# A second k-group by seven products in the second feed-forward, its last weight sum added by a DMA

## The chip, the cores and the metric

The kernel runs on one core of one Trainium2 chip. The metric is the device time of one execution in microseconds, the median over several runs; before the change it is 2688.29 us (three runs, 2687.02 to 2688.56). Engine names are those of the profile: PE is TensorE, DVE is VectorE, ACT is ScalarE, POOL is GpSimd, and SP is the engine whose queue issues the weight loads.

## The reference, cut to what matters

The program is two transformer-like blocks on one sequence of 256 tokens with width 2048, all in float32: sliding-window attention and a SwiGLU feed-forward; then a gated hybrid mixer, a cross attention and a second feed-forward, and a last norm. The change touches the up side of both feed-forwards. In the first:

```
silu(h @ w_gate) * (h @ w_up)        # then @ w_down
```

In the second, `w_up` holds both halves (2 x 5632 columns), a causal three-tap convolution over the tokens comes between, and the halves are then gated:

```
u = h @ w_up
u = causal_conv(u, conv_w) + conv_b
gate, val = u[..., :D_FF_2], u[..., D_FF_2:]
(silu(gate) * val) @ w_down
```

So each feed-forward needs, for one block of 512 columns, two products with the same activations: a left one (gate) and a right one (up, or val), each for two halves of 128 tokens. That is a 2 x 2 arrangement of outputs, and if the sum over the 2048 inputs is cut in two as well, a 2 x 2 by 2 x 2 matrix product.

## The kernel before, in words

**Tiles.** The weights stand in HBM as units of 1 MB: 512 inputs (four k-tiles of 128 rows) by 512 columns. The 2048 inputs are four k-groups of 512, numbered 0 to 3; a unit is one k-group of one column block. SP loads units in a fixed order (`plan`) into four buffers (`RAW = 4`), each loaded again once its last reader is done. A float32 product is made of three passes of a narrower type, so each weight is split first: half a unit (128 x 1024 elements) goes through ACT (`wh`, line 235, a cast) and then DVE (`wl`, line 236, the remainder). Such a split half is a task. Tasks are written three ahead of PE (`AHEAD = 3`), and there are five buffers each for `wh` and `wl` (`WBUF = 5`), so the cast of a task waits until PE is done with the task five before it. `mm` (lines 276 to 282) issues three matmuls with a moving size of 512 columns for each product of one k-tile.

**Seven products.** `pair` computes the left and the right column block together. A normal k-group there takes two units, four tasks and 48 matmuls. For the k-groups listed in `SEVEN1` (first feed-forward) and `SEVEN2` (second) the four half units b11, b21 (left) and b12, b22 (right) and sums of them make seven tasks of two k-tiles and 42 matmuls, as in Strassen's scheme with few additions. The sums of weights are made in place by `form` on DVE, the sums of activations once by `differences`, and the sums of results by the `add` calls in `pair` after the last such group (index 3). The seven products are numbered 0 to 6 here, as `form`'s index `i`. Product 6 uses b21 after its sum, product 2 uses b21 as loaded.

**Order.** Each feed-forward has eleven column blocks; the first goes through `gemm`, the other ten through `pair`. Between two calls of `pair` stand four units of the down projection (`ffn_steps`, `PARTS`). Side work (the convolution, transposes, the split of the hidden block) is written as generators that are stepped once per k-tile or product (`tick`). The order on PE is the written one. On ACT, DVE, POOL and SP the compiler's scheduler orders instructions by when it expects them to be ready, so their order in the profile is not always that of the source; once placed, each engine works its queue in order. PSUM has four banks for `acc` (the four outputs p2 to p5 of a pair, or two outputs of a `gemm`), three for `aux` (o1 and o6 of a pair, transposes) and one for `po` (o7). A `gemm` after a pair takes `acc` banks as they come free.

POOL computes only `power` (line 445) before the change and issues no DMA.

Of the kernel before, what the change touches and what calls it, by code (L numbers as in the profile page):

```python
# [14 lines left out]
ALU = mybir.AluOpType  # L15
# [19 lines left out]
WBUF = 5  # L35
AHEAD = 3
PARTS = ((0,), (1, 2), (3, 4), (5, 6), (7, 8), (9, 10))
SEVEN1, SEVEN2 = (1, 3), (3,)
BRANCH = ((0,), (1,), (2, 3))
LEVELS = (64, 32, 16, 8, 4, 2, 1)  # L40

# [42 lines left out]
class _Net:  # L84
# [87 lines left out]
    def plan(self):  # L172
# [13 lines left out]
        def ffn(gate, up, off, down, seven):  # L186
            for c, n, ks in self.ffn_steps():
                if n is not None:
                    add([U(down, n, ks)])
                elif c:  # L190
                    pair(U(gate, c), U(up, c + off), seven)
                else:
                    add([U(gate, c), U(up, c + off)], True)
            add([U(down, n, PARTS[-1]) for n in range(4)])
# [51 lines left out]
    def form(self, u, i):  # L246

        nc = self.nc
        self.load_ahead(u + 2)
        b12, b22, b11, b21 = (self.raws[u + j][:, 2 * i:2 * i + 2] for j in range(2) for i in range(2))  # L250
        if i == 2:
            nc.vector.tensor_sub(b22, b22, b12)
            nc.vector.tensor_sub(b12, b12, b11)
            nc.vector.tensor_add(b11, b11, b22)
        if i == 5:
            nc.vector.tensor_sub(b21, b21, b11)
        return (b22, b11, b21, b11, b12, b22, b21)[i]

    def task(self):

# [40 lines left out]
    def differences(self, acts, seven):  # L301


        nc = self.nc
        out = []
        for g, z in enumerate(acts):
            h, l = z = self.need(z)
            f = self.s4([128, 4, 256])
            nc.vector.tensor_add(f, h.bitcast(F32), l.bitcast(F32))
            p, q = f[:, :, 0:128], f[:, :, 128:256]  # L310
            yield 2
            if g not in seven:
                h, l = (self.s2([128, 4, 128], F32R) for _ in range(2))
                nc.vector.tensor_sub(p, p, q)
                nc.scalar.copy(h, p)
                nc.vector.tensor_sub(l, p, h.bitcast(F32))
            else:
                s = self.s4([128, 8, 128])
                nc.vector.tensor_add(s[:, 0:2], q[:, 0:2], q[:, 2:4])
                nc.vector.tensor_sub(s[:, 2:4], s[:, 0:2], p[:, 0:2])  # L320
                nc.vector.tensor_sub(s[:, 4:6], p[:, 0:2], q[:, 0:2])
                nc.vector.tensor_sub(s[:, 6:8], p[:, 2:4], s[:, 2:4])
                yield 1
                h, l = (self.s4([128, 8, 128], F32R) for _ in range(2))
                nc.scalar.copy(h, s)
                nc.vector.tensor_sub(l, s, h.bitcast(F32))
            out.append((h, l))
            yield 2
        return out

    def pair(self, left, right, acts, diffs, seven):

        nc = self.nc
        add = nc.vector.tensor_add
        acts = [self.need(z) for z in acts]
        p2, p4, p5, p3 = (self.bank(tag="acc") for _ in range(4))  # L340
        used = set()

        def product(o, z, k, t, stop):
            h, l = self.task()
            for i in range(2):
                self.mm(o, z, k + i, t, (h[:, i], l[:, i]), id(o) not in used, stop and i == 1)
                used.add(id(o))
            self.tick()

        o1 = None  # L350
        for g in range(len(acts)):
            A, S = acts[g], diffs[g]
            if g not in seven:
                for units in (right, left):
                    outs = ((p2, A, 0), (p4, A, 1)) if units is left else ((p5, A, 1), (p3, S, 0))
                    for k, w in enumerate(self.weights(units[g])):
                        for o, z, t in outs:
                            self.mm(o, z, k, t, w, id(o) not in used, False)
                            used.add(id(o))
                        self.tick()  # L360
                continue
            assert self.stream[self.used:self.used + 2] == [right[g], left[g]]
            self.used += 2
            if o1 is None:
                o1, o6, o7 = self.bank(), self.bank(), self.bank(tag="po")
            end = g == seven[-1]
            product(p3, S, 6, 0, end)
            product(o1, A, 0, 0, end)
            if end:
                u, a, b, c = (self.s2([128, 512]) for _ in range(4))  # L370
                nc.scalar.copy(u, o1)
            product(p2, A, 2, 0, end)
            if end:
                add(a, p2, u)
                yield a
            product(o6, S, 2, 0, end)
            if end:
                add(u, o6, u)
            product(p5, S, 0, 0, end)
            if end:  # L380
                add(b, p5, u)
                add(b, p3, b)  # L382
                yield b
            product(o7, S, 4, 0, end)
            if end:
                add(u, o7, u)
            product(p4, A, 2, 1, end)
        add(c, p4, u)
        add(u, p5, u)
        yield c  # L390
        yield u


    def group(self):
# [937 lines left out]
```

## Time and profile before

| | |
|---|---|
| median of three runs | 2688.29 us |
| the profiled execution's own time | 2686.66 us |
| its span, first to last instruction | 2684.5 us |
| TensorE clock granted, mean | 0.999 |
| PE busy | 2657.9 us (99%) |
| DVE busy | 1890.7 us (70%) |
| ACT busy | 1424.2 us (53%) |
| POOL busy | 27.1 us (1%) |
| DMA, mean | 186 GB/s |

The profiled execution is one run; its span is 2.2 us shorter than its time. A busy PE in this profile is not PE at its peak, since matmul records overlap: a 512-column matmul is shown with 390 ns, and the step from one start to the next is what counts. Idle time of an engine that is not the bottleneck costs nothing.

### The profile page before, as it was taken

What the parts mean: (1) busy time and instruction counts of PE and PEld (TensorE: products, weight loads), DVE (VectorE), ACT (ScalarE), POOL (GpSimd) and SP (SyncE); (2) the same over time, 40 slices, a digit from 0 to 9 for tenths busy, and PEclk for the clock granted to TensorE, in tenths of its full rate; (3) what the DMA queues carried; (4) which work ended last, traced back from release to release, by engine and by line L of the source; (5) the groups of instructions that cost most, each with busy time, mean ns of one, the idle gap of its engine ahead of it and who ended that gap; (6) DMA issues with size and microseconds to landing.
All of it is one profiled execution on the core that took longest, in us unless ns stands there. A gap on an engine that the chain in (4) does not pass through costs nothing.

```text
span 2684.5 us, 31592 instructions
## 1 busy us (share of the span) xinstructions
PE 2657.9 (99%) x12352; PEld 2195.2 (82%) x12352; DVE 1890.7 (70%) x2225; ACT 1424.2 (53%) x1849; POOL 27.1 (1%) x27
## 2 busy tenths in 40 slices
PE   8999999999999999999999999999999999999998
PEld 7778888888888888888888888888878888888887
DVE  7775799888888864655545555454578877777776
ACT  6555555555555555454444555444555655555554
POOL 0100000000000000000000000000000000000000
PEclk9999999999999999999999999999999999999999
DMA  7334455555555554445555566444554555555553
GB/s 304 113 126 145 169 218 187 205 192 206 209 195 200 194 187 178 151 172 188 188 190 193 183 225 212 172 157 168 183 180 175 190 193 194 192 190 195 194 193 138
DMA packets 74086, 499.61 MB, mean 186 GB/s; under 512 B 8496, under 2 KB 9392, under 8 KB 14928
## 3 DMA queue, kind: packets, MB, share of 16 engines
q1 hardware_dynamic: 73936, 497.59, 51.4%
q8 instruction: 97, 1.59, 0.2%
q14 instruction: 53, 0.43, 0.0%
HBM read 495.46 MB, written 2.10 MB: 185 GB/s over the span
## 4 chain that ended last, share of the span: by engine, by line
PE 97%; DVE 2%; ACT 1%; POOL 0%; DMA 0%; issue 0%; SPq 0%; POOLq 0%; DVEq 0%; ACTq 0%
PE acc L280 29%; PE acc L282 29%; PE acc L281 29%; PE aux L421 2%; PE aux L282 1%; PE aux L281 1%; PE aux L280 1%; PE po L734 1%; PE po L282 1%; PE po L281 1%; PE po L280 1%; PE aux L969 0%; POOL sm L445 0%; DVE wl L236 0%; DMA raw<-in_w_qkv 0%; PE aux L695 0%
## 5 line engine op out<-in xcount | busy, mean ns | idle before, releaser
L236 DVE TENSOR_TENSOR wl<-raw,wh 128x1024 fp32r<-128x1024 f32 (+1 forms) x1012 | 1230.7, 1220 | 689.0 <-ACT wh L235 677.1
L235 ACT CAST wh<-raw 128x1024 fp32r<-128x1024 f32 (+1 forms) x1012 | 1060.2, 1051 | 1084.0 <-PE acc L282 1020.6
L280 PE MATMUL acc<-wh,s 128*128 128x512 f32 x3440 | 1364.1, 397 | 7.4 <-ACT wh L235 5.5
L282 PE MATMUL acc<-wh,s 128*128 128x512 f32 x3440 | 1342.6, 390 | 0.6 <-DVE s L404 0.6
L281 PE MATMUL acc<-wl,s 128*128 128x512 f32 x3440 | 1341.0, 390 | 0.4 <-DVE wl L236 0.4
L280 PEld LDWEIGHTS acc<-wh,s 128*128 128x128 f32 x3440 | 646.9, 188 | 145.5 <-DVE s L382 7.1
L282 PEld LDWEIGHTS acc<-wh,s 128*128 128x128 f32 x3440 | 646.2, 188 | 138.1 <-DVE s L404 1.1
L281 PEld LDWEIGHTS acc<-wl,s 128*128 128x128 f32 x3440 | 647.3, 188 | 128.2 <-DVE wl L236 1.7
L467 DVE TENSOR_TENSOR x<-acc,x 128x512 f32<-128x512 f32 x112 | 72.8, 682 | 0.0
L421 PEld LDWEIGHTS aux<-con,s 128*128 128x128 f32 x408 | 50.2, 140 | 15.7 <-issue 4.0
L421 PE MATMUL aux<-con,s 128*128 128x128 f32 x408 | 60.9, 272 | 1.8 <-DVE s L1162 1.8
L1159 ACT ACTIVATE s<-aux,vec 128x256 f32<-128x256 f32 x88 | 47.9, 560 | 12.5 <-PE aux L421 7.8
L403 ACT CAST s<-aux 128x512 fp32r<-128x512 f32 x66 | 38.4, 584 | 28.9 <-PE aux L421 18.6
L445 POOL TENSOR_TENSOR sm<-sm,mhalf 128x2 f32<-128x2 f32 (+3 forms) x22 | 26.0, 1182 | 2651.0 <-DVE sm L453 2314.1
L404 DVE TENSOR_TENSOR s<-aux,s 128x512 fp32r<-128x512 f32 x66 | 44.6, 687 | 11.5 <-ACT s L403 10.3
L408 ACT ACTIVATE s<-aux,vec 128x256 fp32r<-128x256 f32 x80 | 37.7, 473 | 22.3 <-PE aux L421 14.2
L280 PE MATMUL aux<-wh,s 128*128 128x512 f32 x120 | 46.7, 389 | 0.0
L281 PE MATMUL aux<-wl,s 128*128 128x512 f32 x120 | 46.7, 389 | 0.0
L282 PE MATMUL aux<-wh,s 128*128 128x512 f32 x120 | 46.7, 389 | 0.0
L409 DVE SCALAR_TENSOR_TENSOR s<-aux,vec,s 128x256 fp32r<-128x256 f32 x80 | 38.3, 482 | 6.5 <-ACT s L408 5.3
L1160 DVE SCALAR_TENSOR_TENSOR s<-aux,vec,s 128x255 f32<-128x255 f32 x88 | 41.0, 478 | 2.4 <-ACT s L1159 0.2
L1162 DVE SCALAR_TENSOR_TENSOR s<-aux,vec,s 128x254 f32<-128x254 f32 x88 | 40.0, 477 | 1.1
(195 smaller groups left out, 1309.1 us busy)
## 6 DMA issues: line engine op xcount, KB each, us to landing
raw<-in_w_up SPq DMA_DIRECT2D x132, 1024.0 KB, 4.8
raw<-in_w_dn SPq DMA_DIRECT2D x88, 1024.0 KB, 4.8
raw<-in_w_in SPq DMA_DIRECT2D x64, 1024.0 KB, 4.8
raw<-in_w_gate SPq DMA_DIRECT2D x44, 1024.0 KB, 4.8
raw<-in_w_ckv SPq DMA_DIRECT2D x32, 1024.0 KB, 4.7
raw<-in_w_qkv SPq DMA_DIRECT2D x19, 1024.0 KB, 5.4
raw<-in_w_o SPq DMA_DIRECT2D x16, 1024.0 KB, 4.7
raw<-in_w_br SPq DMA_DIRECT2D x16, 1024.0 KB, 4.7
```

The source lines that it names most:

```text
L235: nc.scalar.copy(h[:, m], raw[:, m])
L236: nc.vector.tensor_sub(l[:, m], raw[:, m], h[:, m].bitcast(F32))
L280: nc.tensor.matmul(o, ah[:, k, s], h, start=first, stop=False)
L281: nc.tensor.matmul(o, ah[:, k, s], l, start=False, stop=False)
L282: nc.tensor.matmul(o, al[:, k, s], h, start=False, stop=last)
L403: nc.scalar.copy(h[:, k0:k0 + n], src)
L404: nc.vector.tensor_sub(l[:, k0:k0 + n], src, h[:, k0:k0 + n].bitcast(F32))
L421: self.nc.tensor.transpose(b[:, j, t * 128:t * 128 + 128], srcs[t][:, (k + j) * 128:(k + j) * 128 + 128], self.ident)
L467: nc.vector.tensor_add(xs[t], pss[t], xs[t])
L1159: nc.scalar.activation(y[:, j], b[:, j], AF.Identity, bias=bb, scale=w2)
L1160: nc.vector.scalar_tensor_tensor(y[:, j, 1:256], b[:, j, 0:255], w1, y[:, j, 1:256], op0=ALU.mult, op1=ALU.add)
L1162: nc.vector.scalar_tensor_tensor(y[:, j, 2:256], b[:, j, 0:254], w0, y[:, j, 2:256], op0=ALU.mult, op1=ALU.add)
```

## The change

- `SEVEN2` becomes `(1, 3)`: in the second feed-forward k-group 1 goes by seven products too, as it did in the first.
- `form` makes its sums with plus signs: b22 gets b12 added, b12 gets b11 added (index 2), then b11 gets the new b22 added (now at index 3). The last sum, b21 plus the new b11, is no DVE instruction any more but a DMA issued by POOL that adds b11 into b21, both in SBUF (128 x 1024 float32, 512 KB). This holds for both feed-forwards.
- The order of the products 4 and 5 changes: now o7 (with b22) is product 4 and p5 (with b12) is product 5; p5 was product 4 before.
- `differences` has other signs. The sums of results have other signs, and the last of them are ordered anew: after p5 come b, b with p3, u with o7, d; after p4 one sum remains where there were two.

```diff
-SEVEN1, SEVEN2 = (1, 3), (3,)
+SEVEN1, SEVEN2 = (1, 3), (1, 3)
...
         if i == 2:
-            nc.vector.tensor_sub(b22, b22, b12)
-            nc.vector.tensor_sub(b12, b12, b11)
+            nc.vector.tensor_add(b22, b22, b12)
+            nc.vector.tensor_add(b12, b12, b11)
+        if i == 3:
             nc.vector.tensor_add(b11, b11, b22)
-        if i == 5:
-            nc.vector.tensor_sub(b21, b21, b11)
-        return (b22, b11, b21, b11, b12, b22, b21)[i]
+            nc.gpsimd.dma_start(b21, b11, accum_op=ALU.add)
+        return (b22, b11, b21, b11, b22, b12, b21)[i]
...
                 s = self.s4([128, 8, 128])
-                nc.vector.tensor_add(s[:, 0:2], q[:, 0:2], q[:, 2:4])
+                nc.vector.tensor_sub(s[:, 0:2], q[:, 0:2], q[:, 2:4])
                 nc.vector.tensor_sub(s[:, 2:4], s[:, 0:2], p[:, 0:2])
                 nc.vector.tensor_sub(s[:, 4:6], p[:, 0:2], q[:, 0:2])
-                nc.vector.tensor_sub(s[:, 6:8], p[:, 2:4], s[:, 2:4])
+                nc.vector.tensor_add(s[:, 6:8], p[:, 2:4], s[:, 2:4])
...
-                u, a, b, c = (self.s2([128, 512]) for _ in range(4))
+                u, a, b, d = (self.s2([128, 512]) for _ in range(4))
...
+            product(o7, S, 4, 0, end)
             product(p5, S, 0, 0, end)
             if end:
-                add(b, p5, u)
+                nc.vector.tensor_sub(b, p5, u)
                 add(b, p3, b)
                 yield b
-            product(o7, S, 4, 0, end)
-            if end:
                 add(u, o7, u)
+                nc.vector.tensor_sub(d, p5, u)
             product(p4, A, 2, 1, end)
-        add(c, p4, u)
-        add(u, p5, u)
-        yield c
+        add(u, p4, u)
         yield u
+        yield d
```

## Rows read from the trace of the kernel before

**Rows 1.** The page's first part: busy time, share, instructions of each engine.
```profile
PE 2657.9 (99%) x12352; PEld 2195.2 (82%) x12352; DVE 1890.7 (70%) x2225; ACT 1424.2 (53%) x1849; POOL 27.1 (1%) x27
```

**Rows 2.** Waits, whole execution: who <- for whom, us in total, times, longest.
```profile
PEld acc L280 <- DVE s L382: 7.1, 20, 0.4
```

**Rows 3.** Busy us (instructions) PE, PEld, DVE, ACT, POOL, clock, DMA: one period each.
```profile
747.20:810.90 63.70, 63.70 (x286) 52.50 (x285) 54.55 (x54) 34.20 (x35) 0.00 (x0) 1.00 0.53 198
2235.90:2301.90 66.00, 66.00 (x299) 54.38 (x298) 52.42 (x64) 37.03 (x44) 0.00 (x0) 1.00 0.53 192
```

**Rows 4.** Timeline of PE (start us, us): product 1, then the down projection.
```profile
2203.85 0.39 PE L280 MATMUL aux<-wh,s 128*128 128x512 f32 x1
...
2212.01 0.39 PE L280 MATMUL acc<-wh,s 128*128 128x512 f32 x1
```

**Rows 5.** DVE groups in one period of the second feed-forward: busy, mean ns.
```profile
L236 DVE TENSOR_TENSOR wl<-raw,wh 128x1024 fp32r<-128x1024 f32 x27 | 32.7, 1221 | 12.7 <-ACT wh L235 12.5
...
L256 DVE TENSOR_TENSOR raw<-raw 128x1024 f32<-128x1024 f32 x1 | 1.2, 1225 | 0.0
```

**Rows 6.** Timeline of DVE: k-group 3 of one pair, second feed-forward.
```profile
2198.96 1.22 DVE L236 TENSOR_TENSOR wl<-raw,wh 128x1024 fp32r<-128x1024 f32 x1
...
2207.45 1.22 DVE L236 TENSOR_TENSOR wl<-raw,wh 128x1024 fp32r<-128x1024 f32 x1
...
2210.32 0.69 DVE L381 TENSOR_TENSOR s<-acc,s 128x512 f32<-128x512 f32 x1
2210.91 1.22 DVE L236 TENSOR_TENSOR wl<-raw,wh 128x1024 fp32r<-128x1024 f32 x1
2212.05 0.69 DVE L382 TENSOR_TENSOR s<-acc,s 128x512 f32<-128x512 f32 x1
...
2213.25 1.22 DVE L236 TENSOR_TENSOR wl<-raw,wh 128x1024 fp32r<-128x1024 f32 x1
```

**Rows 7.** Timeline of ACT, the same group: casts of tasks 6 to 9.
```profile
2205.89 2.00 ACT L235 CAST wh<-raw 128x1024 fp32r<-128x1024 f32 x2
...
2208.41 2.18 ACT L235 CAST wh<-raw 128x1024 fp32r<-128x1024 f32 x2
```

**Rows 8.** Timeline of SP's queue, the same pair: weight loads issued.
```profile
2186.03 5.73 SPq L215 DMA_DIRECT2D raw<-in_w_dn  x2
...
2206.72 2.30 SPq L215 DMA_DIRECT2D raw<-in_w_dn  x2
```

**Rows 9.** Timeline, first feed-forward, k-group 1: split of task 2, cast and product 6.
```profile
627.03 1.22 DVE L236 TENSOR_TENSOR wl<-raw,wh 128x1024 fp32r<-128x1024 f32 x1
...
633.53 1.05 ACT L235 CAST wh<-raw 128x1024 fp32r<-128x1024 f32 x1 [0.30 <-PE aux L282]
...
638.73 0.39 PE L280 MATMUL acc<-wh,s 128*128 128x512 f32 x1
```

**Rows 10.** Timeline, second feed-forward: first tasks of k-group 1, DVE and PE.
```profile
2305.82 2.36 DVE L236 TENSOR_TENSOR wl<-raw,wh 128x1024 fp32r<-128x1024 f32 x2
...
2312.82 0.39 PE L280 MATMUL acc<-wh,s 128*128 128x512 f32 x1
```

**Rows 11.** DMA issues: count, KB each, median us from issue to landing.
```profile
raw<-in_w_up SPq DMA_DIRECT2D x132, 1024.0 KB, 4.8
...
out<-x SPq DMA_DIRECT2D x8, 256.0 KB, 2.4
...
s<-in_g_final SPq DMA_DIRECT2D x2, 512.0 KB, 6.9
```

**Rows 12.** Timeline of POOL: three of its `power` instructions.
```profile
35.95 0.70 POOL L445 TENSOR_TENSOR sm<-sm,mhalf 128x2 f32<-128x2 f32 x1 [35.51 <-DVE sm L453]
...
85.85 2.54 POOL L445 TENSOR_TENSOR sm<-sm,mhalf 128x8 f32<-128x8 f32 x1 [26.17 <-DVE sm L614]
...
97.98 1.64 POOL L445 TENSOR_TENSOR sm<-sm,mhalf 128x8 f32<-128x8 f32 x1 [9.59 <-DVE sm L614]
```

**Rows 13.** DVE groups around the second feed-forward's `differences`: busy, mean ns.
```profile
L319 DVE TENSOR_TENSOR s<-s 128x256 f32<-128x256 f32 x1 | 0.4, 419 | 0.0
```

## Prediction

> **What bounds the kernel now.** I read the page's busy shares first: PE is at 99%, DVE at 70%, ACT at 53%, POOL at 1% [rows 1]. Then the waits, to see whether anything holds PE: the wait that recurs is for the sum of line 382, twenty times, 7.1 us in all and never over 0.4 us [rows 2]. Then one period (a pair and the four units of the down projection behind it) of each feed-forward: PE is busy through all of both, 63.7 us in the first and 66.0 us in the second, at full clock, while DVE has 54.55 and 52.42 us of work in them [rows 3]. So time falls only if PE gets fewer matmuls, or DVE, ACT or the new DMA comes to hold PE up. How far that is away is read from the timelines of single groups.
>
> **What is removed on PE.** From the first matmul of product 1 to the first of the down projection there are six products of six matmuls, 36 starts in 2212.01 - 2203.85 = 8.16 us, 0.2267 us each and 1.36 us a product [rows 4]. A normal k-group in a pair takes 48 matmuls, a group by seven products 42. Ten pairs lose six each: 60 x 0.2267 = 13.6 us, all on the path.
>
> **DVE and ACT, second feed-forward.** Per pair the new group has seven tasks in place of four: three more splits of 1.22 us. Sums of weights: four on DVE before, twice three now. That is five more instructions, 5 x 1.22 = 6.1 us [rows 5], so DVE goes from 52.4 of 66.0 to 58.5 of 64.6 us, 91%; ACT gets three casts of 1.05 us. In the first feed-forward DVE loses two sums a pair, to 52.1 of 63.7. PE waits for no DVE total there, so that gains nothing; the sums of results stay seven. I cost the totals at nothing, since splits run ahead of PE by up to five tasks; what is late next is local, below.
>
> **The accumulating DMA.** POOL can issue it when task 2 is split (it reads b21) and the third sum is made; product 6's cast waits for its landing, and behind that cast stand all later casts in ACT's queue, behind task 6's split all later DVE work. What is the room?
> - Group 3, both feed-forwards, 20 groups: task 2's split ends at 2198.96 + 1.22 = 2200.2, task 6's cast starts at 2205.89 [rows 6, 7]: 5.7 us. Its split started at 2207.45, 0.5 us after that cast's end. So 6.2 us cost nothing. Beyond that the DVE chain up to line 382 slides, and PE already waits for its end [rows 2]: a late microsecond costs one.
> - Group 1, first feed-forward, 10 groups: task 2's split ends at 628.25 and its cast of task 6 starts at 633.53, 5.3 us; but PE begins product 6 only at 638.73 [rows 9], so with 2.3 us for cast and split the DMA may take 8.2 us.
> - Group 1, second feed-forward, 10 groups: here DVE still works off the convolution. It begins the group's splits at 2305.82, PE begins the group at 2312.82 [rows 10]. Six instructions must pass (three splits, three sums) at 1.18 to 1.22 us, so the DMA starts at about 2313.0; product 6 is due at 2312.82 + 6 x 1.36 = 2320.98, less 2.3: the room is 5.7 us.
>
> How long it takes, no row shows; there is no DMA from POOL and none that adds. From below: a store of 256 KB, half the bytes and no second operand, lands in 2.4 us [rows 11], so not under 3. From above: two passes of a 1 MB load, 2 x 4.8, and the longest POOL instruction shown for making the transfer, 2.5 [rows 11, 12]: 12.1 us. I take the nearest: 512 KB of source and 512 KB of destination are read, the bytes of one 1 MB load, 4.8 us, and 0.7 us on POOL as its shortest instruction [rows 11, 12]: 5.5 us. It should not meet other transfers: in group 3 the loads before it are issued by 2191.8 and land 4.8 us later, the next is issued at 2206.72 [rows 8]. Two loads of 512 KB took 6.9 us each [rows 11]. At 5.5 us the cost is nothing; at 3 too; at 12.1 it is 20 x 5.9 + 10 x 6.4 + 10 x 3.9 = 221 us. POOL's queue holds nothing else there that anyone waits for.
>
> The Trainium skill prices this too: its page "DMA: Bandwidth & Descriptors", section "Anatomy of one DMA — SWDGE (gpsimd) path", gives about 2.0 us plus the bytes over 436 GB/s. By it, an estimate, 512 KB take 3.2 us, or 4.4 with both operands counted, and the sum would stay as it is.
>
> **Sums of results.** p5 moves from product 4 to 5, 1.36 us later, and the second bank of the down projection hangs on b with p3. PE ends product 5 at about 2210.7 and wants the bank at 2212.01 + 0.68 = 2212.7; before, line 382 ended at 2212.05 + 0.69 = 2212.74. Now DVE can put task 8's split where line 381 stood, at 2210.32 (its cast is done by 2209.5), then the two sums: 2211.5 to 2212.75 [rows 6, 7]. The same wait, cost nothing; it has no slack. If the wait of rows 2 went, at most its 7.1 us would be gained.
>
> **`differences`, once.** Group 1's form makes four sums of 0.42 us and one of 1.22 where two of 0.68 were [rows 6, 13]: 1.5 us more on DVE. Between 0 and 1.5 us; I take 0.8.
>
> **Sum.** 13.6 - 0.8 = 12.8 us off the profiled execution's 2686.66 (span 2684.5 and 2.2 around it): 2673.9. The median lies 1.6 us higher: 2675.5, say 2676.
>
> **Rivals.**
> - *The sum lands late (slower).* One mechanism: task 6 waits, ACT and DVE stand behind it, and line 382's successor comes late to PE. With X us from issue to landing the loss is 20 x (X - 6.2) + 10 x (X - 5.7), and it decides from X = 6.5, where it eats the 12.8. At X = 7.3 it is 38 us: 2714. For it: two loads of 512 KB took 6.9 us [rows 11], and adding may not run at the rate of a load. Against: the DMA engines are free there.
> - *DVE holds up POOL while it makes the transfer.* The same `power` instruction of 128x8 took 1.64 us once and 2.54 another time [rows 12], so something on this core can delay POOL by 0.9 us. Then X is 6.4, the loss 20 x 0.2 + 10 x 0.7 = 11, and the time about 2687. The Trainium skill, "SBUF — State Buffer", section "Who interferes with whom", has the cause: a DVE instruction with two SBUF inputs contends with a GpSimd instruction that reads SBUF, not with one that only writes. The rows of `power`, which reads, would fit its first half; whether making descriptors counts as writing only, no row shows.
> - *A split gets between the sums.* If the scheduler puts task 9's split ahead of b with p3 (its cast is done by 2210.6 [rows 7]), the bank comes at 2213.9, 1.15 us later, in 20 pairs: 23 us, 2698.6. Against: before, both line 382 and the sum after it went ahead of that split, which came at 2213.25 [rows 6].
> - *It doesn't do what it says*: DVE at 91% falls behind in the second feed-forward wherever a wait leaves it idle, and PE stands 1 to 2 us a pair: 2686 to 2696.
>
> **How the numbers follow.** The forecast has 0.50; the late sum 0.20; POOL held up 0.15; the split between 0.10; DVE behind 0.05. A change under 0.2% (5.4 us) can't be told from none. Faster takes the forecast and a third of POOL's case, 0.55; same, half of POOL's and edges of the others, 0.14; slower the rest, 0.31. The forecast's own range is 2668 (the old wait gone) to 2681 (X at 6.0 to 6.2 in places). To hold 8 in 10 it must reach into the late sum, to X of 7.2: 2712; below 2668 no term reaches.
>
> **What would show it.** PE periods of 64.6 us in the second feed-forward and 63.7 in the first, no new wait of PE. POOL to landing under 5.7 us. In each group of seven, ACT's cast of task 6 not waiting for a DMA, or by less than 0.5 us. Line 382's successor ending within 0.1 us of PE's need. DVE at 58.5 us a period. The prediction is wrong if PE waits behind task 6, or if the landing takes over 6.5 us; and the gain itself is mis-sized if the step between matmuls is no longer 0.227 us.

## The result, and the profile after it

The changed kernel takes 2707.19 us (median of 4 runs, 2706.48 to 2709.59) against 2688.36 us for the kernel before (2687.02 to 2688.56): ratio 1.0073, interval 1.0055 to 1.009. It is slower by 18.8 us, where 12.8 us less was forecast. The profiled execution took 2706.85 us, its span is 2705.1 us and the mean granted clock 0.999, as before; the clock has a small part in it, 1.6 us in one place, told below. From line 390 or so on, line numbers are one lower than before.

The first part of the page after (it answers [rows 1]):

```profile
PE 2649.4 (98%) x12292; PEld 2184.4 (81%) x12292; DVE 1920.6 (71%) x2258; ACT 1450.5 (54%) x1879; POOL 62.0 (2%) x67
```

The 60 matmuls are gone, and with them 8.5 us of PE's busy time. The span is 20.6 us longer all the same: PE now stands more often. The waits of PE and of its weight loads, whole execution (who <- for whom, us in total, times, longest), say where; they answer [rows 2]:

```profile
PEld acc L280 <- DVE s L383: 33.1, 20, 2.2
...
PE acc L280 <- DVE s L383: 24.6, 20, 1.8
...
PE aux L420 <- DVE s L1161: 4.5, 3, 1.7
```

Line 383 is `add(b, p3, b)`, line 382 of before. The wait for it still comes 20 times, once a pair, but up to 2.2 us (1.8 by PE's own row) where it was never over 0.4. The third row has grown too, from 1.8 us in one wait before: transposes of the convolution, held by VectorE. Next the periods, which answer [rows 3] (busy us and instructions of PE, PEld, DVE, ACT, POOL, clock, DMA share, GB/s): one of the first feed-forward, one of the second, and one short one of the second, from its pair 2 to pair 3, which was not looked at before the prediction:

```profile
737.85:802.71 64.86, 63.80 (x285) 52.51 (x284) 52.24 (x52) 34.28 (x35) 1.74 (x2) 1.00 0.61 210
2257.36:2323.56 66.20, 64.76 (x294) 53.26 (x292) 57.90 (x69) 39.70 (x47) 1.72 (x2) 1.00 0.62 207
2059.71:2118.57 58.86, 54.64 (x247) 44.05 (x246) 52.46 (x65) 35.50 (x44) 1.72 (x2) 1.00 0.58 197
```

The first feed-forward, whose matmuls did not change, takes 1.16 us more a period. In the second, 64.6 us were forecast; PE has 64.76 us of busy time in a period of 66.20. The third row has the same stretch in the kernel before beside it here:

```profile
2047.16:2102.30 55.14, 55.14 (x254) 45.35 (x252) 47.62 (x59) 32.89 (x41) 0.00 (x0) 1.00 0.52 191
```

There PE had no idle time, and six matmuls less should have made it 53.8 us. It takes 58.86, with 52.46 us of work on VectorE.

What happens at a pair's end is seen in the timeline of DVE (start us, us, line, operation, times in a row), group 3 of one pair; it answers [rows 6]:

```profile
2427.31 2.35 DVE L236 TENSOR_TENSOR wl<-raw,wh 128x1024 fp32r<-128x1024 f32 x2
2429.58 0.68 DVE L382 TENSOR_TENSOR s<-acc,s 128x512 f32<-128x512 f32 x1
2430.18 1.21 DVE L236 TENSOR_TENSOR wl<-raw,wh 128x1024 fp32r<-128x1024 f32 x1
2431.32 0.68 DVE L383 TENSOR_TENSOR s<-acc,s 128x512 f32<-128x512 f32 x1
```

and in that of PE at the same place, which answers [rows 4]:

```profile
2430.37 0.39 PE L281 MATMUL acc<-wl,s 128*128 128x512 f32 x1
2430.60 0.39 PE L282 MATMUL acc<-wh,s 128*128 128x512 f32 x1
2432.05 0.50 PE L280 MATMUL acc<-wh,s 128*128 128x512 f32 x1 [1.06 <-DVE s L383]
2432.39 0.39 PE L281 MATMUL acc<-wl,s 128*128 128x512 f32 x1
```

The matmul of 2432.05 is the first into the down projection's second bank, p3's old one. By the step of 0.2267 us it was due at 2430.83; it starts 1.22 us late, when the sum of line 383 is done. Between the two sums of b stands a split (2430.18). Without it line 383 would have ended at about 2430.9.

The accumulating DMA, the page's row of its issues and two of POOL's instructions (they answer [rows 11, 12]):

```profile
raw<-raw POOLq DMA_DIRECT2D x40, 512.0 KB, 4.5
```

```profile
2400.76 0.86 POOL L256 DMA_DIRECT2D raw<-raw  x1 [45.95 <-DVE raw L255]
2419.69 0.86 POOL L256 DMA_DIRECT2D raw<-raw  x1 [18.07 <-DVE wl L236]
```

In the median it lands 4.5 us after its issue: under the 5.5 us that I took and the room of 5.7 to 8.2 that I gave it; 38 of the 40 take 4.48 to 4.81 us, the longest 6.37. In the main the forecast feared the wrong part of the change. But in five of the 20 groups 3 ScalarE's cast of task 6 waits 0.7 to 1.1 us for this landing, as in pair 1 of the second feed-forward:

```profile
2041.41 2.00 ACT L235 CAST wh<-raw 128x1024 fp32r<-128x1024 f32 x2 [1.03 <-DMA raw<-raw]
...
2048.98 0.50 PE L280 MATMUL acc<-wh,s 128*128 128x512 f32 x1 [1.74 <-DVE s L383]
```

In these five the sum of line 383 comes 0.4 to 0.7 us later still than in the pair above, 2.9 us in all (pairs 1, 2, 3 and 5 of the second feed-forward, where the DMA is issued later against PE, and pair 9 of the first, where it takes the 6.37 us).

From the starts of the first matmul of a unit the time can be laid out by stage. The start-up (first weights) differs by up to 2 us from one profiled execution to the next, in every kernel, and is left out. A pair here is the stretch from its first product to that of the next pair; pairs 1 and 2 have two units of the down projection behind them, the others four. Pair 10 has no next pair and is left out.

| us | before | changed | difference |
|---|---|---|---|
| first feed-forward and what lies ahead of it | 970.15 | 982.33 | +12.2 |
| the stages between, and the second feed-forward's first column block | 1003.79 | 1003.79 | 0 |
| second feed-forward, pair 1 | 58.72 | 59.33 | +0.6 |
| pair 2 | 55.13 | 58.86 | +3.7 |
| pair 3 | 67.55 | 72.96 | +5.4 |
| pairs 4 to 9, each | 66.04 | 65.8 (one 66.2) | -0.2 |

In pair 3 of the changed kernel the clock was lower for a short while (the same columns as in the periods above):

```profile
2168.30:2172.00 3.70, 3.70 (x11) 2.89 (x10) 3.61 (x5) 2.15 (x3) 0.00 (x0) 0.54 0.73 259
```

For most of this stretch the trace grants the lower of the clock's two levels, 1.2 GHz, and the matmuls step 0.43 us instead of 0.227: 1.6 of pair 3's 5.4 us. 1.5 us before it, PE had ended a wait of 1.78 us for line 383; in pair 2 it waited 1.70 us there and kept the clock, so what brought it down is not shown. The profile of the kernel before has no such place outside its first and last microseconds.

Two questions follow. Is it the order of the two sums (and not the DMA) that costs over 1 us a pair? And what takes the rest of the 9.7 us in the second feed-forward's first three pairs?

### The profile page after: what moved, and what is told of

It is laid out like the page before. It is cut to its first block, busy times and chain, and to the rows that moved or that the text cites. A ratio compares the mean times of both kernels' runs of the same rounds, so it can differ in the third digit from the quotient of the medians.

```text
span 2705.1 us, 31717 instructions
## 1 busy us (share of the span) xinstructions
PE 2649.4 (98%) x12292; PEld 2184.4 (81%) x12292; DVE 1920.6 (71%) x2258; ACT 1450.5 (54%) x1879; POOL 62.0 (2%) x67
## 4 chain that ended last, share of the span: by engine, by line
PE 85%; DVE 8%; issue 3%; DMA 2%; ACT 1%; POOL 0%; SPq 0%; DVEq 0%; POOLq 0%; ACTq 0%
PE acc L280 26%; PE acc L282 25%; PE acc L281 25%; DVE wl L236 4%; PE aux L420 2%; DMA raw<-raw 2%; PE aux L282 1%; PE aux L281 1%; PE aux L280 1%; ACT wh L235 1%; PE po L733 1%; DVE s L378 1%; DVE s L382 0%; DVE s L383 0%; PE aux L968 0%
## 5 line engine op out<-in xcount | busy, mean ns | idle before, releaser
L236 DVE TENSOR_TENSOR wl<-raw,wh 128x1024 fp32r<-128x1024 f32 (+1 forms) x1042 | 1259.9, 1219 | 680.9 <-ACT wh L235 669.5
L235 ACT CAST wh<-raw 128x1024 fp32r<-128x1024 f32 (+1 forms) x1042 | 1081.6, 1050 | 1058.5 <-PE acc L282 924.1
L280 PE MATMUL acc<-wh,s 128*128 128x512 f32 x3360 | 1333.7, 397 | 31.8 <-DVE s L383 24.6
L282 PE MATMUL acc<-wh,s 128*128 128x512 f32 x3360 | 1311.9, 390 | 0.6 <-DVE s L403 0.6
L281 PE MATMUL acc<-wl,s 128*128 128x512 f32 x3360 | 1311.0, 390 | 1.6 <-DVE wl L236 1.6
L280 PEld LDWEIGHTS acc<-wh,s 128*128 128x128 f32 x3360 | 632.2, 188 | 168.3 <-DVE s L383 33.1
L282 PEld LDWEIGHTS acc<-wh,s 128*128 128x128 f32 x3360 | 631.6, 188 | 135.7 <-DVE s L403 1.1
L256 POOL DMA_DIRECT2D raw<-raw x40 | 34.8, 870 | 1258.3 <-DVE wl L236 692.4
L281 PE MATMUL aux<-wl,s 128*128 128x512 f32 x160 | 62.6, 391 | 0.4 <-DVE wl L236 0.4
L282 PE MATMUL aux<-wh,s 128*128 128x512 f32 x160 | 62.3, 389 | 0.0
L280 PE MATMUL aux<-wh,s 128*128 128x512 f32 x160 | 62.3, 389 | 0.0
L1158 ACT ACTIVATE s<-aux,vec 128x256 f32<-128x256 f32 x88 | 47.7, 560 | 13.6 <-PE aux L420 7.8
L255 DVE TENSOR_TENSOR raw<-raw,raw 128x1024 f32<-128x1024 f32 x40 | 48.9, 1223 | 1.1
L252 DVE TENSOR_TENSOR raw<-raw 128x1024 f32<-128x1024 f32 x40 | 48.9, 1222 | 1.0
```

The costliest lines, as they stand in the source:

```text
L235: nc.scalar.copy(h[:, m], raw[:, m])
L236: nc.vector.tensor_sub(l[:, m], raw[:, m], h[:, m].bitcast(F32))
L252: nc.vector.tensor_add(b22, b22, b12)
L280: nc.tensor.matmul(o, ah[:, k, s], h, start=first, stop=False)
L281: nc.tensor.matmul(o, ah[:, k, s], l, start=False, stop=False)
L282: nc.tensor.matmul(o, al[:, k, s], h, start=False, stop=last)
```

## The experiments

Theory A: p3's bank is freed too late, since the sum that frees it waits for p5, which comes one product later, and a split stands in between. Theory B: the accumulating DMA. Theory C: VectorE has too much to do. All runs were timed in turn with the kernel before.

**1. p3's sum ahead of p5's**

```
             add(u, o6, u)
+            nc.vector.tensor_sub(b, p3, u)
...
-            nc.vector.tensor_sub(b, p5, u)
-            add(b, p3, b)
+            add(b, p5, b)
```

> The changed kernel (2707.2 us), with the sum that reads p3 moved ahead: b = p3 - u right behind u += o6, and b += p5 where b += p3 stood. Nothing else differs, the number of sums included. Theory A (the end of each of the 20 pairs waits for p3's bank, which the changed order of products frees one product later, with a split queued between the two sums): TensorE's wait of 24.6 us over 20 on the sum that reads p3 goes, and the time falls by about that, to 2681 to 2685 us. Theory B (the loss comes from the accumulating DMA, which ScalarE awaits 22 times): no bank decides, the time stays within 3 us of 2707. Theory C (DVE is behind everywhere, whatever it is asked first): the wait moves to the next bank, p5's, and at most 8 us come back, 2699 or more.

Measured: 2676.65 us (2676.12 to 2677.30), 0.996 of before (0.9948 to 0.9973). Line 383's wait is gone from the list. DVE and PE of the same group as above in this kernel:

```profile
2402.12 1.21 DVE L236 TENSOR_TENSOR wl<-raw,wh 128x1024 fp32r<-128x1024 f32 x1
2403.26 0.68 DVE L379 TENSOR_TENSOR s<-acc,s 128x512 f32<-128x512 f32 x1
2403.86 1.21 DVE L236 TENSOR_TENSOR wl<-raw,wh 128x1024 fp32r<-128x1024 f32 x1
2404.99 0.68 DVE L383 TENSOR_TENSOR s<-acc,s 128x512 f32<-128x512 f32 x1
```

```profile
2405.64 0.39 PE L280 MATMUL acc<-wh,s 128*128 128x512 f32 x1
2405.86 0.39 PE L281 MATMUL acc<-wl,s 128*128 128x512 f32 x1
2406.09 0.39 PE L282 MATMUL acc<-wh,s 128*128 128x512 f32 x1
2406.32 0.39 PE L280 MATMUL acc<-wh,s 128*128 128x512 f32 x1
```

and a period of its second feed-forward:

```profile
2235.27:2299.74 64.47, 64.47 (x294) 53.34 (x293) 57.82 (x69) 39.46 (x47) 1.72 (x2) 1.00 0.62 212
```

The splits stand between the sums as before, but the sum that reads p3 (line 379) ends at 2403.94, 1.7 us before PE wants the bank (2405.64), and PE runs through at 0.227 us a matmul. One line of code moved gives 30.5 us, and the kernel is faster than before by 10.8. Theory A holds, and B and the strong form of C fall as the main cause: DVE has the same 57.8 us of work in a period in which PE now has no idle time.

**2. The old order of products, everything else changed**

```
-        return (b22, b11, b21, b11, b22, b12, b21)[i]
+        return (b22, b11, b21, b11, b12, b22, b21)[i]
...
-            product(o7, S, 4, 0, end)
             product(p5, S, 0, 0, end)
...
                 yield b
+            product(o7, S, 4, 0, end)
+            if end:
                 add(u, o7, u)
```

> The changed kernel with the order of products of the kernel before (p5, then o7), its two sums behind p5; the plus signs, the accumulating DMA and the two groups of seven stay. Theory A (p3's bank freed one product later): the slack of one product (1.36 us) is back, the wait at the pairs' ends falls from 24.6 us to about the 7.1 of the kernel before, and the time to about 2707.2 - 17.5 = 2690 us (2685 to 2693). Theory B (the accumulating DMA) and theory C (DVE too full in any order): 2704 to 2709.

Measured: 2684.22 us (2682.27 to 2686.02), 0.9987 of before (0.9978 to 0.9996). PE's own wait for b's second sum falls from 24.6 us to 2.8 in 6 pairs, the six in which ScalarE's cast of task 6 in group 3 waits 0.65 to 1.04 us for the accumulating DMA; a period of the second feed-forward is 64.7 us. It is a little better than A's range and outside that of B and C.

**3. The kernel before with the new order of products only**

```
-        return (b22, b11, b21, b11, b12, b22, b21)[i]
+        return (b22, b11, b21, b11, b22, b12, b21)[i]
...
+            product(o7, S, 4, 0, end)
             product(p5, S, 0, 0, end)
...
-            product(o7, S, 4, 0, end)
-            if end:
                 add(u, o7, u)
```

> The kernel before with one thing of the change alone: product o7 ahead of p5 (and the forms returned in that order), p3's sum behind p5. No DMA sum, minus signs, one group of seven in the second feed-forward. Theory A: the wait for p3's bank at the 20 pairs' ends grows from 7.1 us to some 25 and the time from 2688.4 to about 2706 us (2702 to 2710), slower than before although nothing was added. Theory B (DMA) and C (the second group's work on DVE): within 2 us of 2688.4.

Measured: 2710.82 us (2710.04 to 2712.24), 1.0088 of before (1.0074 to 1.0101): 23.4 us lost by exchanging two products, with no DMA and no second group. Its waits, the same columns as above:

```profile
PEld acc L280 <- DVE s L383: 29.8, 20, 1.5
PE acc L280 <- DVE s L383: 21.3, 20, 1.1
```

and DVE at one pair's end:

```profile
2228.39 0.68 DVE L382 TENSOR_TENSOR s<-acc,s 128x512 f32<-128x512 f32 x1
2228.99 1.21 DVE L236 TENSOR_TENSOR wl<-raw,wh 128x1024 fp32r<-128x1024 f32 x1
2230.12 0.68 DVE L383 TENSOR_TENSOR s<-acc,s 128x512 f32<-128x512 f32 x1
```

It is the same picture as in the changed kernel. All 20 pairs are alike here: in each the matmul that waits for line 383 starts 1.2 us late. The time is 0.8 us above the range that I gave for A, since I took the waits at PE's rows alone.

**4. The changed kernel with one group of seven in the second feed-forward**

```
-SEVEN1, SEVEN2 = (1, 3), (1, 3)
+SEVEN1, SEVEN2 = (1, 3), (3,)
```

> The changed kernel with the second feed-forward's group 1 put back to eight products (one group of seven there, as before); order of products, signs and accumulating DMA stay. Theory A + C (the wait for p3's bank costs the same with one group as with two; the second group saves 13.6 us of matmuls and gives some 8 to 9 back in the first three pairs of the second feed-forward, where the convolution falls into the next pair): 2707.2 + 13.6 - 8.5 = about 2712 us (2709 to 2716). Rival C alone (the second group costs more than it saves): under 2705. Rival without C (it saves all 13.6): 2719 to 2722.

Measured: 2712.03 us (2711.55 to 2713.79), 1.0091 of before (1.0075 to 1.0106), as theory A + C has it. So the second group is worth some 5 us in the changed kernel, not 13.6, and not a loss.

**5. The last sum of weights on VectorE** (from experiment 1)

```
-            nc.gpsimd.dma_start(b21, b11, accum_op=ALU.add)
+        if i == 5:
+            nc.vector.tensor_add(b21, b21, b11)
```

> The first experiment's kernel (p3 first, 2676.7 us), the last sum of weights made on VectorE two forms later, as in the kernel before, instead of by the accumulating DMA. So it tells what the DMA is worth once p3's bank is out of the way. 40 sums of 1.2 us go back to VectorE, which has room in most groups; ScalarE's 29.5 us of waits for the DMA go. Theory A: the time stays within 3 us of 2676.7, with the first three pairs of the second feed-forward (where the DMA lands late behind a late sum and VectorE is full) moving either way by some 2 us. Theory B (the DMA is a cost): 2665 to 2672. Rival (VectorE has no room for them, the DMA is what carries the change): 2682 or more.

Measured: 2676.33 us (2674.73 to 2677.47), the same as experiment 1. ScalarE's waits for the DMA (29.5 us, 22 times) are gone, and VectorE does 40 sums more; neither moves the time. A period is 64.45 us in both. The DMA neither costs nor saves anything here: theory B falls from its other side too. This is the kernel in which p3's bank is free 1.7 us early; the 2.9 us that the DMA's landing adds in the changed kernel, where nothing is to spare, it can't show.

**6. The DMA one form later** (from experiment 1)

```
+        if i == 4:
             nc.gpsimd.dma_start(b21, b11, accum_op=ALU.add)
```

> The first experiment's kernel (p3 first, 2676.7 us), the accumulating DMA issued one form later (the sum that it adds stays where it was). It measures the room that the DMA has. In the first experiment's trace the split of the sum's weights ends 1.99 us ahead of its product in group 3, 2.89 in group 1 of the first feed-forward and 0.7 in group 1 of the second. If the DMA is what sets those leads, an issue one task (1.4 to 2 us) later costs about 1 us in each of the second feed-forward's 10 groups 1 and next to nothing elsewhere: 2684 to 2692 us. If the casts ahead of it set the leads, the DMA has the room: within 2 us of 2676.7.

Measured: 2675.52 us (2674.87 to 2676.99), no change. But it settles nothing on the room: POOL issues the DMA at the same place, at 2394.23 us against 2394.49 in experiment 1, the whole execution being 0.27 us ahead. What releases it is VectorE's sum and split, not the place of the call. Inconclusive.

**7. The convolution earlier** (from experiment 1)

```
-            yield 3 if c == 0 else 8
+            yield 3 if c < 4 else 8
```

> The first experiment's kernel (p3 first, 2676.7 us), the convolution of pairs 1 to 3 of the second feed-forward started after 3 steps instead of 8, so that it lies in the two down projections behind its pair and not in the next pair's first groups. Theory C (there VectorE has the convolution's 10 us and group 1's three sums at once; the pairs 1 to 3 lost 2.0 + 1.9 us at the transposes and the 1.36 us of group 1 twice): about 6 us come back, 2669 to 2672 us. Rival (the loss moves to the down projections, whose additions and splits then stand behind the convolution): within 2 us of 2676.7, or more.

Measured: 2680.97 us (2678.81 to 2682.50), 4.3 us more than experiment 1: a miss. Three steps behind the pair the rows are not scaled yet (line 1203 scales them), and the transposes wait for ScalarE instead:

```profile
PE aux L420 <- ACT s L1203: 5.6, 3, 1.9
```

**8. The kernel before with p3's sum first**

```
                 add(u, o6, u)
+                add(b, p3, u)
...
-                add(b, p5, u)
-                add(b, p3, b)
+                add(b, p5, b)
```

> The kernel before (2687.5 us) with p3's sum ahead of p5's (b = p3 + u behind u += o6, b += p5 behind p5), nothing else changed. It tells how much of the gain of the first experiment is open to the old kernel: its wait of 7.1 us over 20 at the same bank. By the shifts of the first experiment against before (0.23 us a pair) 4.6 us come back: 2681 to 2684 us. Rival (the old wait costs all of its 7.1 us and a slow restart): 2678 to 2681. Rival (something else holds the pair's end): 2686 to 2688.

Measured: 2687.28 us (2686.00 to 2689.08), ratio 1.0 (0.9991 to 1.0009). Nothing, as the last rival had it, but not for its reason. The pairs tell: each is 0.23 us shorter, as expected (pairs 4 to 9: 65.8 for 66.04), except pairs 2 and 3, which are 1.8 us longer. Their transposes wait, in a kernel with no group 1 by seven:

```profile
PE aux L421 <- DVE s L1162: 5.5, 3, 1.8
```

So this wait is not made by group 1's sums. On ScalarE and VectorE the planner (the compiler's scheduler) has set the convolution's work among the splits in another order than before, and the fourth set of transposes finds its bank (there are three) still unread.

**9. Transposes two steps apart** (from experiment 1)

```
-                yield 1
+                yield 2 if 0 < c < 4 else 1
...
-                yield 1
+                yield 2 if 0 < c < 4 else 1
```

> The first experiment's kernel (p3 first, 2676.7 us), the convolution's four sets of transposes of pairs 1 to 3 set two steps apart instead of one. In the first experiment's trace the fourth set waits 1.8 us for a bank that VectorE has still to read, and the pairs 2 and 3 each start their group 0 2.0 us later against before. Theory C1 (the transposes come faster than VectorE can read their banks): those waits go, 2 x 2.0 = 4 us, 2671 to 2674 us. Rival C2 (VectorE has too much work in these short pairs, whatever the order): the wait turns up at group 1's splits instead, 2676 to 2679.

Measured: 2674.70 us (2673.26 to 2675.28), 0.9951 of before (0.9937 to 0.9965). The transposes of pair 1's convolution, in PE's timeline, ahead of pair 2's group 1, in the changed kernel:

```profile
2063.02 0.60 PE L420 MATMUL aux<-con,s 128*128 128x128 f32 x4
2066.67 0.63 PE L420 MATMUL aux<-con,s 128*128 128x128 f32 x4 [1.66 <-DVE s L1161]
```

and in this one:

```profile
2051.06 0.60 PE L420 MATMUL aux<-con,s 128*128 128x128 f32 x4
2054.27 0.60 PE L420 MATMUL aux<-con,s 128*128 128x128 f32 x4
```

That wait is gone, and pairs 2 and 3 take 1.05 us less each, not 2.0: group 1 behind it waits longer for its splits, which takes most of the rest. Both theories have a part.

**10. As 9, from step 5** (from experiment 9)

```
-            yield 3 if c == 0 else 8
+            yield 3 if c == 0 else 5 if c < 4 else 8
```

> As the experiment before this one (transposes of pairs 1 to 3 two steps apart), and started at step 5 instead of 8: late enough for ScalarE's last scaling of the rows (it came 3 steps in, where the earlier start at step 3 met it), early enough to be out of the way of group 1's sums and splits. C1: 2670 to 2673 us, with part of the 1.4 us of group 1 back in pairs 2 and 3. C2 (VectorE too full in any order): 2676 to 2680.

Measured: 2678.12 us (2674.83 to 2678.45), not better than 9: pair 2 takes 57.24 us where 9 has 55.98. Moving the convolution only moves the lateness, which is C2's side.

**11. Without group 1's sums in pairs 1 to 3** (from experiment 1)

```
-        if i == 2:
+        short = self.stream[u][0] == "w_up2" and self.stream[u][1] in (12, 13, 14) and self.stream[u][2] == 1
+        if i == 2 and not short:
...
-            nc.vector.tensor_add(b11, b11, b22)
+            if not short:
+                nc.vector.tensor_add(b11, b11, b22)
```

> The first experiment's kernel (p3 first, 2676.7 us) without VectorE's three sums of weights in group 1 of pairs 1 to 3 of the second feed-forward (9 instructions of 1.2 us left out, so these weights are wrong; products, splits and DMA stay). It tells how much of what these pairs give back is due to group 1's sums. By the table of pairs of the first experiment (57.1 us from pair 2 to 3 where before had 55.1 and 1.6 less was due): if the sums are the cause of both losses (C2), 3 x 2 to 7 us come back, 2669 to 2671. If the transposes' wait is the planner's order and not the sums' (C1; in the kernel before with p3 first the same 1.8 us appeared with no group 1), only group 1's own 1.4 us a pair: 2672 to 2674. Neither: 2676 to 2678.

It leaves these nine sums out, so it tells of time only. Measured: 2669.86 us (2669.32 to 2672.88). The three pairs take 2.2, 1.5 and 1.5 us less than in experiment 1, 5.1 in all; the rest of the 6.8 is mostly this execution's earlier start (1.2 us in the profile). The transposes still wait in pairs 2 and 3 (3.7 us in all); in pair 1 that wait is gone with the sums. So the total is that of C2 and the picture that of C1: in pairs 2 and 3 the two losses are separate, the transposes by the planner's order, group 1 by three sums that stand in VectorE's queue behind the convolution.

**12. Those sums on POOL** (from experiment 9)

```
+        short = self.stream[u][0] == "w_up2" and self.stream[u][1] in (12, 13, 14) and self.stream[u][2] == 1
+        eng = nc.gpsimd if short else nc.vector
         if i == 2:
-            nc.vector.tensor_add(b22, b22, b12)
-            nc.vector.tensor_add(b12, b12, b11)
+            eng.tensor_add(b22, b22, b12)
+            eng.tensor_add(b12, b12, b11)
         if i == 3:
-            nc.vector.tensor_add(b11, b11, b22)
+            eng.tensor_add(b11, b11, b22)
```

> The experiment with the spaced transposes (2674.7 us), with the three sums of group 1 in pairs 1 to 3 of the second feed-forward made by POOL, which is busy 2% of the span, instead of VectorE: 9 instructions move, the sums stay as they are. Leaving them out gave 5.1 us in these pairs. No row of this case has a POOL sum of 128x1024; its nearest rows take 0.95 us (a memset of that size) and 0.7 to 2.6 us (a power of 128x2 to 128x8), so a sum may take 1 to some 5 us. If group 1 in these pairs is late only by VectorE's queue (sums standing behind the convolution), 4 to 5 us come back: 2669 to 2671. If POOL's sums are slow (3 x 4 us or more, one after another) the casts wait for POOL instead: 2673 to 2680. If VectorE is held up while POOL adds (its instructions beside them take longer): 2676 or more, with longer rows of VectorE beside POOL's.

Measured: 2670.04 us (2668.85 to 2670.99), 0.9936 of before (0.9923 to 0.995): the best of the versions that leave nothing out, 17.4 us under the kernel before and 37 under the changed one. Pair 2's period in it, to be read against 58.86 us of the changed kernel and 55.14 of before:

```profile
2042.42:2096.92 54.50, 54.44 (x247) 44.03 (x246) 51.08 (x61) 34.91 (x44) 10.67 (x5) 1.00 0.64 212
```

PE is busy through nearly all of it again, though the period is still 0.7 us over the 53.8 that were due. POOL's three sums there, and VectorE beside them:

```profile
2045.26 2.40 POOL L254 TENSOR_TENSOR raw<-raw 128x1024 f32<-128x1024 f32 x1 [22.31 <-DVE wl L236]
2047.74 3.28 POOL L255 TENSOR_TENSOR raw<-raw,raw 128x1024 f32<-128x1024 f32 x1
2051.09 3.26 POOL L257 TENSOR_TENSOR raw<-raw,raw 128x1024 f32<-128x1024 f32 x1
```

```profile
2045.10 0.47 DVE L1161 SCALAR_TENSOR_TENSOR s<-aux,vec,s 128x255 f32<-128x255 f32 x1
2045.60 0.48 DVE L1163 SCALAR_TENSOR_TENSOR s<-aux,vec,s 128x254 f32<-128x254 f32 x1
2046.56 2.18 DVE L236 TENSOR_TENSOR wl<-raw,wh 128x1024 fp32r<-128x1024 f32 x1 [0.47 <-ACT wh L235]
2048.66 0.86 DVE L1161 SCALAR_TENSOR_TENSOR s<-aux,vec,s 128x255 f32<-128x255 f32 x2
2049.45 0.85 DVE L1163 SCALAR_TENSOR_TENSOR s<-aux,vec,s 128x254 f32<-128x254 f32 x2
2050.23 1.87 DVE L236 TENSOR_TENSOR wl<-raw,wh 128x1024 fp32r<-128x1024 f32 x1
...
2053.58 1.33 DVE L1175 TENSOR_TENSOR s<-s,s 128x512 f32<-128x512 f32 x1
```

The splits beside POOL's sums take 2.18 and 1.87 us for 1.22 [rows 5], line 1175 1.33 us for 0.69, and POOL 3.3 us for 2.4. The convolution's instructions, of whose inputs one is in PSUM, keep their 0.47. So VectorE was held up, as the third expectation said, but by 2 to 3 us a group, less than the three sums that it no longer makes; the three pairs are 4.3 us shorter than in experiment 9, where leaving the sums out had given 5.1.

## Why the prediction was wrong

- **PE's matmuls, -13.6 us: right.** Where nothing holds PE, a period of the second feed-forward went from 66.04 to 64.45 us: 1.36 us by the formula and 0.23 by the old wait (experiment 8 has these 0.23 by themselves). The step between matmuls stayed at 0.227 us.
- **Sums of results, "the same wait, cost nothing; it has no slack": this step failed.** I had the planner put one split where line 381 stood and the two sums back to back behind it. In [rows 6] themselves it does not do so: there a split (2210.91) stands between the sums of lines 381 and 382. After the change it does the same, with p5 one product later, and what was sum, split, sum, just in time, is sum, split, sum, 1.2 us late. The rival "a split gets between the sums" named this mechanism and its price, 1.15 us a pair; measured are 1.13 us a period over before in most pairs, 12.2 us in the first feed-forward. I gave it 0.10 on the ground that line 382 *and the sum after it* went ahead of a split, and overlooked the split ahead of line 382. Experiment 3 shows it with nothing else changed, experiment 1 takes it away.
- **"At most its 7.1 us would be gained": mis-sized at both ends.** The old wait is worth 0.23 us a pair, 4.6 us, by experiment 8. The new one is worth 30.5 us by experiment 1, not the 24.6 us of PE's row: PE also loses at the restart (0.50 us for the first matmul and 0.34 us to the next, where 0.39 and 0.23 are usual). Counted from start to start, the 20 matmuls that wait come 27.8 us late and those behind them 2.2 us more, 30.1 in all. The row of the weight loads, 33.1 us, was the nearer one.
- **DVE's totals, costed at nothing: right for the period read, wrong for three that were not.** 58.5 us of 64.6 were forecast and 57.8 of 64.47 are measured, at no cost (experiments 1 and 5). But pairs 1 to 3 of the second feed-forward have the convolution of the pair before in their first groups; pair 2 has 52.4 us of work on DVE, and without idle time its period would be 53.8, so 97% and not 91%. By the first experiment's kernel against before less 1.59 us a pair, these pairs give back 2.4 + 3 x 1.6 = 7.2 us. Nearly all of it is in pairs 2 and 3, 3.5 us each: 1.5 by group 1's sums in the queue (experiment 11) and 2.0 by the transposes' wait that experiment 11 leaves. Pair 1 gives back only 0.2, since in the kernel before it has such a wait already. I took one steady period [rows 3] for all ten.
- **The accumulating DMA: right in its duration, and all but right in its cost.** 4.5 us to landing in the median, 5.5 forecast. The sign "ACT's cast of task 6 not waiting for a DMA, or by less than 0.5 us" failed: 22 casts waited, 28.9 us in all, 2.7 at most. In 15 of the 20 groups 3 this cost PE nothing, in five the chain that the late-sum rival describes added the 2.9 us told above, part of the 30.1. In these five every landing later than 6.4 us ahead of the time at which PE wants the bank makes the sum of line 383 later by as much. So from its issue the DMA had a room of 5.8 us in the groups 3 of the first feed-forward, but of 4.7 in most of the second and of 3.9 in its pairs 1 to 3, where I had 5.7 to 6.2 for all. Once p3's bank has room, the cost is nothing (experiment 5). By the formula of the Trainium skill, "DMA: Bandwidth & Descriptors", section "Anatomy of one DMA — SWDGE (gpsimd) path", 4.4 us was the estimate with both operands counted, and the trace agrees with its 4.5. The rivals that hung on it, with 0.35 of the chance, fall as the cause of the loss: its instruction takes 0.86 or 0.87 us on POOL in 38 of 40 cases, 1.05 at most. How much room it has in experiment 1's kernel was not measured (experiment 6); in that kernel's group 3 the split behind it ends 1.99 us ahead of its product.
- **`differences`, 0.8 us**: no trace tells it apart from the rest of pair 1.

Together: -13.6 for the matmuls, -4.6 for the old wait, 30.1 for the new one and 7.2 for the short pairs make 19.1 us, where the times differ by 18.8. The measured 2707 us lies inside the wide range of the prediction, which went up to 2712; that is luck, since this end was put there for a late DMA and not for the order of the sums.

So 2676 us, the number forecast, is what experiment 1 measures, 2676.65. That is partly chance: the gain of the old wait (4.6) and the loss of the short pairs (7.2) about cancel. Against the changed kernel the error is the bank, 30.5 of 31.2 us.

Open is what makes the planner order the convolution differently in experiments 1 and 8, and what brought the clock down in pair 3. Group 1's sums on POOL without spacing the transposes was not run; experiment 11, with the sums left out, still has the 2 us at the transposes.

## What to carry to other kernels

When products or instructions are put in another order, follow each PSUM bank to the instruction that frees it: an exchange of two products cost 23 us here with no work added, and making the sum that reads the bank first gave 30 back with no work added. Where the trace shows the planner setting a split between two dependent sums, expect it to do so again. Read an engine's load in the shortest period too, not only in a steady one.

## What the hardware showed that was not expected

- An accumulating DMA of 512 KB from SBUF to SBUF took 4.5 us from issue to landing (median of 40) and 0.87 us of POOL, beside 4.8 us for a 1 MB load [rows 11].
- A sum of 128x1024 float32 takes POOL 2.4 us, VectorE 1.22. Side by side the one that starts second is done only when the other is out of its way, if VectorE's instruction has two inputs in SBUF. In experiment 12 all six splits that met a sum of POOL ended 1.08 us after that sum's end, however early they had started (they took 1.87 to 3.16 us), and the six sums of POOL that met such an instruction already running ended 2.25 to 2.27 us after its end. The Trainium skill, "SBUF — State Buffer", section "Who interferes with whom", has this rule (such an instruction contends with a GpSimd one that reads SBUF, one with a single SBUF input does not), and the rows of experiment 12 agree, the 0.47 us of the convolution's instructions included. They show one engine waiting until the other's whole instruction is done. The kernel before has it too: three of eight `power` instructions of 128x8 took 2.54 to 2.62 us where the others took 1.64 [rows 12]; in these three a split was running, and each ended 1.49 to 1.50 us after the split.
